# Recurrent scan of a hybrid backbone: both directions' hops side by side, the projection's products in one run behind them

## The chip, the cores and the metric

The kernel runs on one core of a Trainium2 chip. The metric is the device time of one execution in microseconds (us); the median of several runs is compared. Four engines matter here: TensorE (PE in the profile) multiplies, VectorE (DVE), ScalarE (ACT) and GpSimd (POOL) work elementwise, and SyncE's queue (SP) issues most DMAs. Every engine works through its own instructions in order and waits at an instruction until what it needs is there.

## The reference, cut to what matters

One layer of a diffusion backbone over 256 context tokens and 2048 latent tokens (2304 in all, width 1024): a token mixer with three head groups fed by one input projection, then a mixture of experts. The stage that changes is the second head group, a bidirectional RWKV-7 recurrence with 4 heads and a 64x64 state for each head:

```python
def step(S, inp):
    r_t, w_t, k_t, v_t, kk_t, a_t = inp
    sa = -jnp.einsum('nhvk,nhk->nhv', S, kk_t)
    S = S * w_t[:, :, None, :] + sa[..., None] * (kk_t * a_t)[:, :, None, :] + v_t[..., None] * k_t[:, :, None, :]
    return S, jnp.einsum('nhvk,nhk->nhv', S, r_t)
...
y = unboth(_rwkv7_scan(both(r, r), both(w_f, w_b), both(k_f, k_b), both(v, v), both(kk, kk), both(a_f, a_b)))
```

The two directions don't depend on each other. Beside it the input projection `u @ w_in` gives the columns of the two other head groups; those columns are needed only after the scan.

## The kernel before

**The scan.** The 2304 tokens are cut into 18 blocks of 128 for each direction, and `run` (line 609) works through 18 pairs of blocks, one of each direction (d = 0 and 1). A block is four chunks of 32 tokens (u = 0 to 3), and a chunk is a dependent chain of three hops, written in `chunk` (line 646). Hop A multiplies with the masked Gram matrix and the state (lines 652 and 654 on PE, tiles rkGK and rkS), and ACT copies the result out of PSUM (lines 658 and 659, tile rkR). Hop B multiplies with the inverse of the chunk's triangular matrix (line 661, rkTb), and ACT copies again (662 and 663, rkuv). Hop C (666 and, where outputs are needed, 672) gives the update of the state, which VectorE adds (668, rkS); the next chunk's hop A needs it. `chain` (line 624) yields after every hop of every direction: 24 times in a block, n = 0 to 23, even n for direction 0 and odd n for direction 1; chunk, hop and direction run with n like digits.

**The preparation** of the next pair of blocks is a generator of 13 pieces, `prep` (line 494), and `PLAN` (line 623) says behind which n how many of them stand: three behind n = 0, one each behind 1 to 6, 21 and 22, two behind 23. On PE these are four Gram products of 8 PE records each (line 563, tiles rkbk and rkar), each read out of PSUM by four VectorE instructions (567 twice, 569, 570), four transposes (581), read by ACT (583, rkBKt), and, behind n = 21 to 23, the products of the inverse (598 twice, 605 twice). All of them share a ring of two PSUM banks, so a product waits until the one two before it has been read out. Between the Gram products and line 598 lies a chain through other engines: POOL adds (572, rkLc), SP stores and loads (573, 504), VectorE solves the triangular systems in 15 steps of two small instructions (513, 514), SP stores and loads again (517, 588), and POOL expands the result (591, rkD).

**The filler products.** Behind each hop `fill` issues some of the projection's products; they need nothing of the scan. `FILL[n//2%3]` is how many: 4 behind hop A, 3 behind B, 4 behind C. They are lines 184 (128x384 results) and, for columns that go by token, 203 (128x256); 24 of them make one result, which ACT and VectorE take out of PSUM (188 or 800 to 808; 207 and 208) and SP stores. The weights are loaded by SP (162) and split by ACT (163) and POOL (164, tile wl). The activations come in thirds, and at the start of a new third they are loaded through POOL's queue (line 145).

**What sets the order.** PE's instructions stand as the program issues them in this stage (`manual_schedule`, line 1756). Those of the other engines, and everything behind the scan, are placed by a scheduler that plans with its own model of the times; a change of PE's order can so move rows on any engine.

Of the kernel before, what the change touches and what calls it, by code (L numbers as in the profile page):

```python
# [460 lines left out]
class Rwkv:  # L461
# [147 lines left out]
    def run(s, L, fill):  # L609

        s.loads(L[0])
        for n,_ in enumerate(s.prep(L[0])): fill(-1,n)
        for i,segs in enumerate(L):
            nxt=L[i+1] if i+1<len(L) else None
            P=iter(())
            if nxt: s.loads(nxt); P=s.prep(nxt)
            K=s.PLAN.copy()
            for n,_ in enumerate(s.chain(segs,i>=2)):
                for _ in range(K.pop(n,0)): next(P,None)
                fill(i,n)  # L620
            for _ in P: pass

    PLAN={0:3,1:1,2:1,3:1,4:1,5:1,6:1,21:1,22:1,23:2}
# [1059 lines left out]
                    s.finish((15-b)*128,f,sm)  # L1683


PRE=250; PREP={7:200}; FILL=(4,3,4)

R0=dict(g=(0,1),mm=(2,3,4),a0=(5,),a1=(6,),c=(7,)); RG=dict(g=(0,1),mm=(2,3),a0=(5,),a1=(6,),c0=(7,),c1=(4,))
LEAD=3; WO=3; EL=8; PRE0=288
def body(tc, I, out, dbg=None, mark=lambda n: None):  # L1690
    nc=tc.nc; es=ExitStack()
    with es:
# [20 lines left out]
        with P('rp') as rp:  # L1713
# [28 lines left out]
          def fill(k):  # L1742
              for _ in range(k):
                  if next(p2,0)==0: return
# [6 lines left out]
        with P('rkc') as rkc, ExitStack() as e2:  # L1751
# [4 lines left out]
            with pr, tc.manual_schedule(engines={mybir.EngineType.PE}):  # L1756
                fill(PRE)
                mark('scan')
# [99 lines left out]
```

## Time and profile before

| | us |
|---|---|
| median of 3 runs | 3917.51 |
| the 3 runs | 3916.85, 3917.51, 3926.28 |
| the profiled execution | 3949.18 |
| its span, first to last instruction | 3947.4 |
| scan with fillers and preparation, 655 to 1415 us of the span | 760 |
| the stage behind it (SSD and GLA head groups), 1415 to 1900 us | 485 |

The profiled execution lasts 31.7 us longer than the median of the runs without a profile; 1.8 us of its time lie outside its span. In the rows of a timeline the first number is the start in us from the span's start, the second the duration, and a bracket at the end gives the idle time of that engine before the row and what ended it. Rows of equal instructions that follow each other are merged, and xN is their count; one product of 32-bit floats in 128 columns shows as two PE records, so hop B is x2.

### The profile page before, as it was taken

The page shows a single profiled execution, that of the slowest core. Times are in us where ns is not written, and L with a number is a line of the kernel's source. Part 1 is how long each engine was busy: PE and PEld are TensorE (multiplying, and loading weights), DVE is VectorE, ACT ScalarE, POOL GpSimd, SP SyncE. Part 2 cuts the span into 40 slices and gives each one's busy share as a digit, 9 for nine tenths or more (in the row PEclk, how much of TensorE's full clock was granted, in tenths as well). Part 3 has the DMA queues.
Part 4 walks back from the last instruction along what each step waited for, and adds up shares of the span by engine and source line. Part 5 has one row for each costly group of instructions (what it writes and reads, how often), then busy time and mean ns, then how long its engine had stood idle before and what let it go on. Part 6 is the DMA issues. An engine that isn't in the chain of part 4 may idle for free. (4 is left out here: it accounts for less than half of the span.)

```text
span 3947.4 us, 66654 instructions
## 1 busy us (share of the span) xinstructions
PE 3525.1 (89%) x23502; PEld 3006.8 (76%) x23502; DVE 2685.3 (68%) x6775; ACT 1706.2 (43%) x3955; POOL 1329.0 (34%) x1224
## 2 busy tenths in 40 slices
PE   8989887999799978995789899999999999999986
PEld 5978777888688857774567678888888887787865
DVE  4576865876777648775899766666666665666658
ACT  3555553545454533444555323343333333333334
POOL 0243543443343310100044533333334343344323
PEclk9999989999899988996899899999999999999988
DMA  7656554333333276864665468788788887888874
GB/s 228 212 184 206 175 152 133 83 100 101 111 92 98 51 223 215 250 186 167 199 194 167 156 172 231 220 251 243 219 241 242 251 235 227 245 242 229 254 210 160
DMA packets 498511, 745.81 MB, mean 189 GB/s; under 512 B 156704, under 2 KB 393312, under 8 KB 469216
## 3 DMA queue, kind: packets, MB, share of 16 engines
q1 hardware_dynamic: 438880, 522.20, 41.0%
q0 software_dynamic: 59296, 219.33, 22.0%
q8 instruction: 187, 3.06, 0.3%
q14 instruction: 148, 1.21, 0.1%
HBM read 524.31 MB, written 217.06 MB: 188 GB/s over the span
## 5 line engine op out<-in xcount | busy, mean ns | idle before, releaser
L1546 POOL DMA_INDIRECT d_f<-yo,en x162 | 346.6, 2140 | 569.4 <-DVE yo L1543 314.0
L1543 DVE SCALAR_TENSOR_TENSOR yo<-mm,f_w,g2r 128x512 f32<-128x512 f32 (+7 forms) x324 | 236.6, 744 | 265.6 <-PE mm L1541 171.2
L1562 POOL DMA_INDIRECT xg<-d_h,en x162 | 232.1, 1433 | 371.8 <-DVE yo L1543 61.6
L184 PE MATMUL b<-uh,wh 128*128 128x384 f32 (+1 forms) x912 | 320.1, 356 | 12.6 <-ACT sce L805 5.2
L184 PE MATMUL b<-ul,wh 128*128 128x384 f32 (+1 forms) x912 | 320.3, 352 | 5.9 <-DMA ul<-d_ul 3.6
L184 PE MATMUL b<-uh,wl 128*128 128x384 f32 (+1 forms) x912 | 320.9, 352 | 0.0
L1445 DVE TENSOR_TENSOR w13l<-raw,w13h 128x2048 fp32r<-128x2048 f32 x102 | 232.8, 2283 | 25.3 <-ACT w13h L1445 25.3
L1445 ACT ACTIVATE w13h<-raw 128x2048 fp32r<-128x2048 f32 x102 | 195.0, 1914 | 104.5 <-DMA raw<-in_exp_w_dram 94.4
L1328 POOL DMA_INDIRECT d_tab<-q_tk,q_slot x128 | 146.9, 1148 | 248.2 <-DVE q_slot L1321 135.7
L1541 PE MATMUL mm<-w2h,hWh 128*128 128x512 f32 (+7 forms) x480 | 202.3, 422 | 13.0 <-DVE yo L1543 12.3
L1512 PE MATMUL a<-w13h,xTh 128*128 128x512 f32 x464 | 190.2, 410 | 9.0 <-ACT xTh L1471 8.4
L1445 DVE TENSOR_TENSOR w2l<-raw,w2h 128x2048 fp32r<-128x2048 f32 x66 | 151.3, 2293 | 68.9 <-ACT w2h L1445 66.0
L1512 PE MATMUL a<-w13l,xTh 128*128 128x512 f32 x464 | 190.4, 410 | 8.0 <-DVE w13l L1445 8.0
L1541 PE MATMUL mm<-w2h,hWl 128*128 128x512 f32 (+7 forms) x480 | 186.9, 404 | 6.8 <-DVE hWl L1504 6.8
L1541 PE MATMUL mm<-w2l,hWh 128*128 128x512 f32 (+7 forms) x480 | 191.2, 399 | 1.6 <-DVE w2l L1445 1.6
L184 PEld LDWEIGHTS b<-uh,wh 128*128 128x128 f32 x912 | 175.9, 194 | 20.2 <-ACT sce L805 6.4
L1512 PE MATMUL a<-w13h,xTl 128*128 128x512 f32 x464 | 187.7, 405 | 0.0
L184 PEld LDWEIGHTS b<-ul,wh 128*128 128x128 f32 x912 | 177.7, 195 | 9.3 <-DVE ul L139 4.0
L184 PEld LDWEIGHTS b<-uh,wl 128*128 128x128 f32 x912 | 177.6, 195 | 1.4
L1445 ACT ACTIVATE w2h<-raw 128x2048 fp32r<-128x2048 f32 x66 | 126.5, 1916 | 116.1 <-DMA raw<-in_exp_w_dram 70.5
L1475 PE MATMUL g<-ident,xg 128*128 128x128 f32 (+9 forms) x1296 | 167.6, 263 | 9.9 <-DMA xg<-d_h,en 5.8
L1475 PEld LDWEIGHTS g<-ident,xg 128*128 128x128 f32 (+9 forms) x1296 | 142.4, 140 | 38.2 <-issue 14.6
(706 smaller groups left out, 10553.8 us busy)
## 6 DMA issues: line engine op xcount, KB each, us to landing
raw<-in_exp_w_dram SPq DMA_DIRECT2D x162, 1024.0 KB
w13h<-in_exp_w_dram SPq DMA_DIRECT2D x30, 1024.0 KB
wr<-in_w_in_dram SPq DMA_DIRECT2D x46, 512.0 KB
uht<-d_uh POOLq DMA_DIRECT2D x32, 512.0 KB
ult<-d_ul POOLq DMA_DIRECT2D x32, 512.0 KB
mrw<-in_ada_w_dram SPq DMA_DIRECT2D x32, 512.0 KB
rkX<-d_ops SPq DMA_DIRECT2D x36, 384.0 KB
rpx<-d_rw SPq DMA_DIRECT2D x54, 192.0 KB
```

Of the source, the lines that this page charges most:

```text
L184: s.nc.tensor.matmul(P.rearrange("p (i t)->p i t",t=128),l,r[:,a//128:,k],start=(i==0),stop=(i==23)); i+=1
L1328: d=s.nc.gpsimd.indirect_dma_start(out=s.S['tab'],out_offset=bass.IndirectOffsetOnAxis(ap=s.slot[:,l,k:k+1],axis=0),in_=s.tk[:,l:l+1],in_o ...
L1445: pin(nc.scalar.activation(H,r,AF.Copy)); pin(nc.vector.tensor_tensor(L,r,rnd(H),op=OP.subtract))
L1475: for k in range(4): nc.tensor.transpose(p[:,k,:m],B['x'][:m,(4*g+k)*128:(4*g+k+1)*128],s.id[:m,:m])
L1512: nc.tensor.matmul(p,a[:,k],b[:,:,k],start=(i==0),stop=(i==23)); i+=1
L1541: nc.tensor.matmul(r[:m],a[:,k],b[:,k,cs],start=(i==0),stop=(i==5)); i+=1
L1543: else: nc.vector.scalar_tensor_tensor(o[:m,cs],r[:m],B['w'] if isinstance(B['w'],float) else B['w'][:m],s.g2[:m,cs],op0=OP.mult,op1=OP.mult)
L1546: d=nc.gpsimd.indirect_dma_start(out=s.S['f'],out_offset=bass.IndirectOffsetOnAxis(ap=B['en'][:m],axis=0),in_=o[:m],in_offset=None,compute ...
L1562: s.nc.gpsimd.indirect_dma_start(out=x[:m],out_offset=None,in_=s.S['h'],in_offset=bass.IndirectOffsetOnAxis(ap=B['en'][:m],axis=0))
```

## The change

The fillers now stand only behind the odd n, that is behind the hop of direction 1, twice as many at a time: 8 behind the two hops A, 6 behind the two hops B, 8 behind the two hops C. Their number in a chunk (22) and in a block (88) is as before. `PLAN` and the pieces of the preparation are as before.

```diff
             for n,_ in enumerate(s.chain(segs,i>=2)):
                 for _ in range(K.pop(n,0)): next(P,None)
-                fill(i,n)
+                if n%2: fill(i,n)
             for _ in P: pass
...
-PRE=250; PREP={7:200}; FILL=(4,3,4)
+PRE=250; PREP={7:200}; FILL=(8,6,8)
```

First place, PE in the 16th block, chunk u = 3, hop A of both directions (652 and 654: the hop; 203: fillers). Before:

```order
L652 MATMUL b_14018<-rkuv_5463,rkGK_13594 64x64 x2
L654 MATMUL b_14018<-rkS_5468,rkar_5447 128x128 x2
L203 MATMUL b_14358<-wh,uh 128x256
L203 MATMUL b_14358<-wl,uh 128x256
L203 MATMUL b_14358<-wh,ul 128x256
L203 MATMUL b_14358<-wh,uh 128x256
L652 MATMUL b_14019<-rkuv_5465,rkGK_13631 64x64 x2
L654 MATMUL b_14019<-rkS_5472,rkar_5449 128x128 x2
```

And after:

```order
L652 MATMUL b_14018<-rkuv_5463,rkGK_13594 64x64 x2
L654 MATMUL b_14018<-rkS_5468,rkar_5447 128x128 x2
L652 MATMUL b_14019<-rkuv_5465,rkGK_13627 64x64 x2
L654 MATMUL b_14019<-rkS_5472,rkar_5449 128x128 x2
L203 MATMUL b_14368<-wh,uh 128x256
L203 MATMUL b_14368<-wl,uh 128x256
L203 MATMUL b_14368<-wh,ul 128x256
L203 MATMUL b_14368<-wh,uh 128x256
```

Direction 1's hop moved up past four fillers; eight now follow.

Second place, PE in the same chunk, from hop B of direction 1 to the second product of line 598 (rkD is what POOL's line 591 makes). Before:

```order
L661 MATMUL b_14021<-rkR_14370,rkTb_13992 128x128
L598 MATMUL b_14434<-rkD,rklf_5455 128x128 x4
L203 MATMUL b_14358<-wh,ul 128x256
L203 MATMUL b_14358<-wh,uh 128x256
L203 MATMUL b_14358<-wl,uh 128x256
L666 MATMUL b_14020<-rkuv_5463,rkBKt_13670 128x128 x2
L672 MATMUL b_14018<-rkuv_5463,rkGK_13594 64x64 x2
L598 MATMUL b_14450<-rkD,rklf_5457 128x128 x4
```

And after:

```order
L661 MATMUL b_14021<-rkR_14361,rkTb_13972 128x128
L598 MATMUL b_14431<-rkD,rklf_5455 128x128 x4
L203 MATMUL b_14368<-wh,ul 128x256
L203 MATMUL b_14368<-wh,uh 128x256
L203 MATMUL b_14368<-wl,uh 128x256
L203 MATMUL b_14368<-wh,ul 128x256
L203 MATMUL b_14368<-wh,uh 128x256
L203 MATMUL b_14368<-wl,uh 128x256
L666 MATMUL b_14020<-rkuv_5463,rkBKt_13663 128x128 x2
L672 MATMUL b_14018<-rkuv_5463,rkGK_13594 64x64 x2
L598 MATMUL b_14450<-rkD,rklf_5457 128x128 x4
```

The three fillers that stood ahead of direction 1's hop B and of the first product of line 598 stand behind it now.

Third place, VectorE in the 8th block (the last third of the activations is loaded there), behind the last read of a Gram product (570). Before:

```order
L570 TENSOR_TENSOR rkGK_10048<-b_10065,mgk_5426 128x512
L549 TENSOR_TENSOR rkbk_5451<-rkX,rkEi 64x4x32 x2
L668 SCALAR_TENSOR_TENSOR rkS_5468<-b_9932,rkG_9459,rkSG_9938 128x64 x2
L549 TENSOR_TENSOR rkbk_5451<-rkX,rkEi 64x4x32 x2
L668 SCALAR_TENSOR_TENSOR rkS_5472<-b_9933,rkG_9489,rkSG_10034 128x64 x2
L533 SCALAR_TENSOR_TENSOR rkA<-rm_5434,rkX 128x128 x2
```

And after:

```order
L570 TENSOR_TENSOR rkGK_10039<-b_10065,mgk_5426 128x512
L533 SCALAR_TENSOR_TENSOR rkA<-rm_5434,rkX 128x128 x2
L549 TENSOR_TENSOR rkbk_5451<-rkX,rkEi 64x4x32 x2
L668 SCALAR_TENSOR_TENSOR rkS_5468<-b_9932,rkG_9459,rkSG_9938 128x64 x2
L549 TENSOR_TENSOR rkbk_5451<-rkX,rkEi 64x4x32 x2
L668 SCALAR_TENSOR_TENSOR rkS_5472<-b_9933,rkG_9489,rkSG_10025 128x64 x2
```

Line 533, which reads a freshly loaded tile (rkX), moved ahead of both directions' updates of the state. In the order of the stage behind the scan some rows of PE, VectorE, ACT and SP stand elsewhere too.

## Rows read from the trace of the kernel before

**Rows 1.** Busy time by stretch: us of the stretch, then for each engine its busy us and its count, the granted clock of TensorE as a share of 2.4 GHz, the DMA share and GB/s.

```profile
655.00:1415.00 760.00, 684.42 (x5349) 609.84 (x5347) 546.00 (x1645) 382.44 (x1240) 286.20 (x392) 0.97 0.34 88
1415.00:1900.00 485.00, 380.61 (x5088) 306.28 (x5089) 336.68 (x829) 199.92 (x532) 41.79 (x82) 0.85 0.70 219
```

**Rows 2.** The waits of PE between 655 and 1415 us: what waited, for what; us in total, times, longest.

```profile
PE b L598 <- POOL rkD L591: 42.5, 13, 18.6
PE b L661 <- ACT rkR L659: 11.6, 11, 3.1
PE b L581 <- DVE rkGK L570: 10.6, 11, 1.8
PE b L563 <- DVE rkTb L607: 3.5, 4, 1.3
```

**Rows 3.** Timeline of PE, a chunk with 128x256 fillers and nothing of the preparation, hop A of both directions.

```profile
1295.14 0.34 PE L652 MATMUL b<-rkuv,rkGK 128*64 128x64 f32 x4
...
1295.87 0.36 PE L203 MATMUL b<-wl,uh 128*128 128x256 f32 x1
...
1296.19 0.28 PE L203 MATMUL b<-wh,uh 128*128 128x256 f32 x1
1296.31 0.28 PE L203 MATMUL b<-wl,uh 128*128 128x256 f32 x1
1296.52 0.34 PE L652 MATMUL b<-rkuv,rkGK 128*64 128x64 f32 x4
```

**Rows 4.** The same with 128x384 fillers.

```profile
1037.91 0.34 PE L652 MATMUL b<-rkuv,rkGK 128*64 128x64 f32 x4
...
1038.64 0.42 PE L184 MATMUL b<-ul,wh 128*128 128x384 f32 x1
1038.90 0.34 PE L184 MATMUL b<-uh,wl 128*128 128x384 f32 x1
1039.08 0.35 PE L184 MATMUL b<-uh,wh 128*128 128x384 f32 x1
...
1039.53 0.34 PE L652 MATMUL b<-rkuv,rkGK 128*64 128x64 f32 x4
```

**Rows 5.** Timeline of PE in the last block, where the fillers have run out and the hops of both directions stand side by side.

```profile
1400.88 0.29 PE L652 MATMUL b<-rkuv,rkGK 128*64 128x64 f32 x4
...
1401.74 0.34 PE L652 MATMUL b<-rkuv,rkGK 128*64 128x64 f32 x4
...
1403.32 0.49 PE L661 MATMUL b<-rkR,rkTb 128*128 128x128 f32 x2 [0.38 <-ACT rkR L659]
```

**Rows 6.** Timeline of PE around the first and the second product of line 598, in four blocks.

```profile
1006.18 2.07 PE L598 MATMUL b<-rkD,rklf 128*128 128x128 f32 x8 [18.55 <-POOL rkD L591]
...
1270.43 0.82 PE L598 MATMUL b<-rkD,rklf 128*128 128x128 f32 x5 [0.71 <-POOL rkD L591]
...
1345.20 1.16 PE L598 MATMUL b<-rkD,rklf 128*128 128x128 f32 x8 [1.45 <-POOL rkD L591]
1346.11 0.36 PE L203 MATMUL b<-wh,ul 128*128 128x256 f32 x1
...
1346.55 0.61 PE L666 MATMUL b<-rkuv,rkBKt 128*128 128x128 f32 x4
...
1388.08 2.08 PE L598 MATMUL b<-rkD,rklf 128*128 128x128 f32 x8 [8.42 <-POOL rkD L591]
```

**Rows 7.** Timelines of PE and VectorE from the first Gram product to the second transpose of a block.

```profile
1352.90 1.95 PE L563 MATMUL b<-rkar,rkbk 128*128 128x128 f32 x16
...
1361.17 0.63 PE L581 MATMUL b<-ident,rkbk 128*128 128x128 f32 x4
...
1353.99 0.57 DVE L567 TENSOR_TENSOR rkLb<-b,mlo 32x128 f32<-32x128 f32 x2 [1.18 <-PE b L563]
...
1360.33 0.69 DVE L570 TENSOR_TENSOR rkGK<-b,mgk 128x512 f32<-128x512 f32 x1
```

**Rows 8.** Timelines of PE and ACT around the products of line 605 in the 7th block: ACT copies the second product of line 598 out (600, rkW), which the second half of the x16 needs.

```profile
948.02 2.17 PE L605 MATMUL b<-rkD,rkW 128*128 128x128 f32 x16
...
948.40 0.58 ACT L600 ACTIVATE rkW<-b 128x512 f32<-128x512 f32 x1
```

**Rows 9.** Timelines of the 8th block, where the last third of the activations is loaded: the SP queue (durations are those of issuing), then VectorE, then PE.

```profile
955.31 0.38 SPq L489 DMA_DIRECT2D rkX<-d_ops  x1
...
956.30 6.28 SPq L162 DMA_DIRECT2D wr<-in_w_in_dram  x1
...
965.73 1.29 SPq L573 DMA_DIRECT2D rkLd<-rkLc  x2
...
960.98 0.48 DVE L668 SCALAR_TENSOR_TENSOR rkS<-b,rkG,rkSG 128x64 f32<-128x64 f32 x2
...
967.92 0.74 DVE L533 TENSOR_TENSOR_SCAN rkA<-rm,rkX 128x128 f32<-128x128 f32 x2 [5.09 <-DMA rkX<-d_ops]
...
969.58 0.49 PE L661 MATMUL b<-rkR,rkTb 128*128 128x128 f32 x2 [3.02 <-ACT rkR L659]
```

**Rows 10.** Timelines of VectorE and POOL: a step of the triangular solve alone, one beside a product of POOL, and that product.

```profile
983.46 0.20 DVE L513 TENSOR_TENSOR rktm<-rkSy,rkTn 64x55 f32<-64x55 f32 x1
...
983.93 2.27 DVE L513 TENSOR_TENSOR rktm<-rkSy,rkTn 64x60 f32<-64x60 f32 x1
...
983.74 2.39 POOL L164 TENSOR_TENSOR wl<-wr,wh 128x1024 fp32r<-128x1024 f32 x1 [12.12 <-issue]
```

## The prediction

> **What bounds the kernel now.** The change touches one stage, so I read that stage first: which engine is busy, and what PE waits for when it isn't. Between 655 and 1415 us PE is busy 684 of 760 us at a granted clock of 0.97, and VectorE 546 us [rows 1]. The reader should see two things: PE is the fullest engine, and about 76 us of the stage are PE's waits. The table of waits then says where these lie [rows 2]: 42.5 us before the products of line 598, 11.6 us before hop B, 10.6 us before the transposes, 3.5 us before the first Gram product of a block. So the hops, which the change brings together, hardly wait: their fillers cover the copies between them. What waits is the preparation of the next block. Line 598 waits 13 times. One of these is a second product of its block (0.71 us) and one lies in the block where the fillers have run out (8.42 us) [rows 6]; in the other 11 cases the first product stands in PE's order before POOL's expansion is done. Eleven of the 16 blocks that have fillers throughout are therefore paced, up to that product, by the chain over VectorE, SP and POOL and not by PE's work; I call them the paced blocks. The 8th block holds the one long wait, 18.55 us [rows 6].
>
> **The change part by part.** The number of products, copies and DMAs is the same; only PE's order is edited, and with it the places that the scheduler gives to the others.
>
> (a) Hops side by side. With 128x256 fillers, from the start of direction 0's hop A to that of direction 1's takes 1296.52 - 1295.14 = 1.38 us, four fillers among them at a step of 1296.31 - 1296.19 = 0.12 us, so 0.90 us without the fillers [rows 3]. With 128x384 fillers it is 1.62 us, and 0.90 us without four at 0.18 us [rows 4]. Where the fillers have run out the same two hops stand 1401.74 - 1400.88 = 0.86 us apart [rows 5]. Going from hop to filler and back thus costs 0.04 us. Of the 12 pairs of hops in a block, 7 become truly adjacent (behind n = 0, 2, 4, 6 and 22 a piece of the preparation still stands between the two), so 7 x 0.04 = 0.28 us a block, 4.5 us over 16 blocks at most. All seven lie ahead of the first product of line 598, so in the paced blocks the wait takes this up; in the 5 others it counts: 1.4 us, and I take **-1.0**, since hops B and C have no 64-column tile at their start and should save less. The bound below is -4.5.
>
> (b) The cover of the copies. Direction 1's copies for hop B queue behind direction 0's on ACT; without fillers that shows as a wait of 0.38 us before direction 1's hop B [rows 5]. Before, four fillers, hop B of direction 0 and three fillers covered them; now eight fillers and that hop. From one hop of a direction to its next there are 6 to 8 fillers and one hop of the other direction, before and after, at 0.12 to 0.18 us each. So the new neighbourhood costs **nothing**, because 8 x 0.12 = 0.96 us hide 0.38. If that cover were gone, it would be 0.38 us in 4 chunks of 16 blocks, 24 us.
>
> (c) Pieces of the preparation behind odd n. They used to follow fillers of the same pair and now come ahead of them: the third Gram product by 4 fillers, the first transpose by 3, the third by 4, the first product of line 598 by 3, both of line 605 by 4. The pieces behind even n keep their place. Gram products and transposes: from the first Gram product to the second transpose passes 8.27 us in a block, and VectorE's reading out fills it from 1353.99 to 1361.02 [rows 7]; the second transpose is what waits (10.6 us in 11 cases [rows 2]) and there are 14 fillers ahead of it before and after. So the third Gram product will wait a little earlier for its bank, and the sum stays; bound 0 to +2.4 (0.15 us in 16 blocks).
>
> The first product of line 598 is different: in the paced blocks it starts when POOL is done, whatever stands ahead of it, and work moved from before it to behind it is added to the block. Three fillers move: 3 x 0.12 = 0.36 or 3 x 0.18 = 0.54 us, 0.45 in the mean (the three that stand behind it already, with the way into hop C, take 1346.55 - 1346.11 = 0.44 us [rows 6]), in 11 blocks: **+4.8** at 0.44, bound 0 if the chain should end earlier by as much. The second product gains these three fillers as cover, so its one wait of 0.71 us shrinks: **-0.4**.
>
> The products of line 605 lose four fillers of distance to the second product of line 598, whose copy by ACT they need. In the 7th block that copy ends at 948.98 and the second half of the x16 starts at about 949.0 [rows 8], so there the 0.48 us are lost, in most blocks not; **+0.5**, bound 0 to +1.
>
> (d) Behind line 605 stand eight fillers where there were four, so the next block's first Gram product comes later against VectorE's reading of its bank: 3.5 us in 4 waits [rows 2], of which up to 0.6 us each go: **-2.4**, bound -3.5.
>
> (e) Other engines. In the 8th block VectorE's order puts line 533 ahead of both updates of the state. It waited 5.09 us for its tile until 967.92 us, while the updates had run at 961 [rows 9]. If the tile lands as late again, the next hop A can start only at about 967.92 + 0.74 + 0.48 us and a small product, 970 us, where before hop B of that chunk came at 969.58, behind a wait of 3.02 us [rows 9]: some 3 us lost. If the tile lands in time, because the order of POOL now has the big load a little later, the 3.02 and 0.4 us behind it go. I take **0**, with -3.4 to +3.
>
> The sum: -1.0 + 4.8 - 0.4 + 0.5 - 2.4 + 0 = **+1.5 us** on the profiled execution's 3949.18, so 3950.7; carried to the median of the runs, 3917.51 + 1.5 = **3919.0**.
>
> One rule of the Trainium skill bears on the chain that paces the blocks. A step of the solve takes 0.20 us; the one that runs beside POOL's product of 2.39 us takes 2.27 us and ends where that product ends [rows 10]. The Trainium skill, SBUF — State Buffer, section SBUF: two separate sides, says that VectorE instructions with two SBUF inputs and GpSimd's share a port pair as an exclusive lock, held for the whole instruction; the trace agrees with it here. By that rule the sum would keep its terms and gain one, the number of such meetings more or fewer times 2.07 us; I leave it at zero and make it a rival.
>
> **The rivals.**
>
> R1, slower: POOL's product meets the solve more often. A meeting lengthens the chain by 2.27 - 0.20 = 2.07 us [rows 10], and in a paced block PE waits all of it. It decides from the point at which line 164 starts while the 15 steps run. For it: POOL's and VectorE's rows are placed anew, with the two updates of the state close together. Against: the scheduler moved few of POOL's rows. One meeting more in half of the paced blocks is 12 us: 3919 + 12 = 3931; in all of them 3942.
>
> R2, faster: the 8th block's long wait shrinks. The stores of line 573 stood on SP behind a weight load that took 6.28 us to issue and left at 965.73 [rows 9]. If they leave with the others, the solve begins about 9 us earlier, and with the wait of 3.02 us some 12 us of the 18.55 + 3.02 go: 3907. Against: the solve also stands behind the fillers' own VectorE work in that block.
>
> R3, either way: the stage behind the scan is laid out anew. PE is idle 485 - 381 = 104 us there [rows 1]; a tenth to an eighth of that won or lost is 10 to 13 us: 3907 or 3931. Nothing in the trace gives the sign.
>
> R4: the edit gives what its shape suggests, 24 runs of fillers becoming 12, each change worth the 0.04 us of (a) with nothing lost at line 598: -4.5 - 2.4, 3911. The paced blocks speak against it; it counts with the forecast, as no measurable change.
>
> **How the numbers follow.** A measurement of this kernel can tell about 0.3% from no change, that is 11.8 us: 3905.8 to 3929.3. The forecast with R4 and the small misses of each term have 0.55. R1 has 0.15 and R3 on that side 0.09: slower 0.24. R2 has 0.13 and R3 on that side 0.08: faster 0.21, the greater part of it close to the edge. The range adds the bounds: below -4.5 - 3.5 - 3.4 and a part of R2 or R3, 3902; above 4.8 + 2.4 + 1 + 3 and R1 in half the blocks or R3, 3939. R1 in all blocks and a loss of all cover lie outside.
>
> **What would show it.** Steps (a) and (b): two hops A 0.86 us apart, and waits before hop B not above some 15 us in all. Step (c): line 598 still the longest wait, 45 to 50 us in about 12 cases, and some waits now at line 605 and at the third Gram product. Step (d): the waits of line 563 for rkTb near 1 us. The stage would end at 1415 + 1.5 us. The prediction is wrong if hop B's waits grow to tens of us (the cover of (b) was misjudged), if line 598's waits change by more than 10 us (R1, R2), or if the stage behind the scan changes its length by as much (R3).

## The result, and the profile after

The changed kernel takes 3968.77 us in the median of 4 runs (3963.17 to 3991.37), the kernel before 3921.90 us beside it: the ratio is 1.0131, 95% interval 1.0086 to 1.0175, 47 us slower. The prediction was 3919 with a range up to 3939.

The same two stretches as in [rows 1], after (the scan, then the stage behind it; columns as there):

```profile
649.70:1426.70 777.00, 690.99 (x5347) 619.59 (x5346) 545.32 (x1643) 382.59 (x1239) 285.02 (x392) 0.95 0.33 86
1426.70:1924.30 497.60, 387.55 (x5089) 312.20 (x5087) 337.13 (x827) 201.04 (x532) 41.79 (x82) 0.82 0.68 214
```

The scan is 17.5 us longer than before (759.55, from the first hop to the last) and the stage behind it 12.8 us longer (484.80). PE's waits in the scan, as in [rows 2]:

```profile
PE b L598 <- POOL rkD L591: 58.8, 14, 25.9
PE b L581 <- DVE rkGK L570: 10.8, 11, 2.6
PE b L666 <- ACT rkuv L663: 7.2, 6, 3.2
PE b L661 <- ACT rkR L659: 3.9, 11, 0.5
```

Line 598 has 16 us more than before, hop B (661) 8 us less, and hop C (666), which waits for the copies behind hop B, 7.2 us instead of 3.1. Where no piece of the preparation stands, a chunk can take as long as before: here the one that answers to [rows 3], PE's timeline from its first hop A to that of the next chunk.

```profile
1306.18 0.34 PE L652 MATMUL b<-rkuv,rkGK 128*64 128x64 f32 x4
...
1307.09 0.34 PE L652 MATMUL b<-rkuv,rkGK 128*64 128x64 f32 x4
...
1312.88 0.34 PE L652 MATMUL b<-rkuv,rkGK 128*64 128x64 f32 x4
```

It takes 1312.88 - 1306.18 = 6.70 us; before, the same chunk (from 1295.14) took 6.68. The scan's loss is to be looked for where the preparation stands. By groups of blocks (1 to 7, the 8th, 9 to 16), a second execution of the kernel before:

```profile
654.20:949.40 295.20, 274.47 (x2123) 247.46 (x2122) 220.49 (x672) 153.34 (x493) 122.62 (x165) 0.97 0.33 83
949.40:1014.50 65.10, 42.58 (x313) 37.84 (x312) 33.17 (x95) 20.52 (x66) 21.06 (x30) 0.79 0.54 165
1014.50:1352.10 337.60, 317.44 (x2499) 282.79 (x2498) 262.10 (x756) 177.69 (x571) 133.94 (x187) 0.99 0.33 83
```

And after:

```profile
649.70:954.70 305.00, 276.29 (x2122) 250.61 (x2121) 222.13 (x673) 152.93 (x493) 121.96 (x165) 0.97 0.32 81
954.70:1020.40 65.70, 39.71 (x315) 35.76 (x314) 30.14 (x94) 21.66 (x69) 20.64 (x29) 0.79 0.53 163
1020.40:1365.50 345.10, 324.21 (x2497) 290.23 (x2496) 261.71 (x754) 176.83 (x568) 134.29 (x187) 0.98 0.32 81
```

The loss is spread: 9.8 us in the first seven blocks, most of it idle time of PE, 0.6 in the 8th, 7.5 in the blocks 9 to 16, most of it busy time at a lower granted clock.

The start of the first product of line 598 parts each of the 17 blocks that hold a preparation in two. Summed over these blocks, by the starts in the traces, 612.2 us lie ahead of it and 128.3 from it to the block's end in the second execution of the kernel before; in the changed kernel 616.3 and 142.1, in its second execution 620.3 and 142.2. So 13.9 us of the scan's loss lie behind that product in both executions, and 4.1 and 8.1 ahead of it. Most blocks have 0.3 to 0.9 us more behind it, the 2nd has 1.8, the 4th and the 11th have 2.9 each. Chunk by chunk (each from its first hop A to that of the next), the changed kernel's two executions take -0.7 and -0.4 us more in the first chunks of these blocks, 1.4 and 1.8 in the second, -4.2 and -4.2 in the third, 21.7 and 25.1 in the fourth, which holds lines 598 and 605. The 11th block grew most, from 44.8 to 50.9 us (49.6 in the second execution). Its first product of line 598, and the stretch from there to its end in the columns of [rows 1], in the kernel before (second execution):

```profile
1138.31 1.16 PE L598 MATMUL b<-rkD,rklf 128*128 128x128 f32 x8 [1.72 <-POOL rkD L591]
...
1138.31:1145.82 7.51, 7.51 (x59) 6.89 (x60) 5.97 (x13) 4.16 (x12) 3.74 (x5) 1.00 0.33 86
```

And after:

```profile
1146.65 2.08 PE L598 MATMUL b<-rkD,rklf 128*128 128x128 f32 x8 [3.74 <-POOL rkD L591]
...
1146.65:1157.04 10.39, 10.39 (x63) 9.61 (x63) 4.47 (x14) 4.21 (x12) 4.00 (x6) 0.75 0.19 50
```

Behind the longer wait a part of the stretch ran at the lower of TensorE's two clock levels, 1.2 GHz; before, all of it ran at 2.4 GHz.

**A table for what follows.** From the traces: the scan (first hop A to last hop C), the stage behind it, and the router's stretch behind that (first product of line 1237 to the last of line 1366: the output projection and the choice of experts), in us. The first row of results is the kernel before, run again (e1_before_again); each ratio is to the kernel before on the same chip.

| run | ratio | scan | stage | router |
|---|---|---|---|---|
| kernel before | | 759.55 | 484.8 | 371 |
| e1_before_again | 0.9995 (0.998 to 1.001) | 759.06 | 486.3 | 370 |
| changed kernel | 1.0131 (1.0086 to 1.0175) | 777.06 | 497.6 | 373 |
| e6_after_again | 1.0135 (1.0113 to 1.0158) | 781.15 | 499.5 | 387 |
| e2_pieces_back | 1.0088 (1.0062 to 1.0115) | 783.42 | 492.1 | 373 |
| e3_pieces_only | 1.0090 (1.0063 to 1.0118) | 787.26 | 497.5 | 361 |
| e4_pairs_lean | 1.0134 (1.0108 to 1.0159) | 778.80 | 499.2 | 400 |
| e5_one_block | 1.0045 (1.0028 to 1.0062) | 759.14 | 498.4 | 374 |
| e12_other_block | 1.0038 (1.0021 to 1.0055) | 759.85 | 494.2 | 387 |
| e8_products_first | 1.0138 (1.0118 to 1.0158) | 766.75 | 494.3 | 405 |
| e7_weights_first | 1.0136 (1.0114 to 1.0159) | 783.86 | 494.1 | 391 |
| e9_weights_ahead | 1.0131 (1.0103 to 1.0159) | 774.25 | 492.2 | 391 |
| e11_fifth_block | 1.0019 (1.0001 to 1.0036) | 772.85 | 480.0 | 368 |
| e10_l598_back | 1.0088 (1.0061 to 1.0114) | 777.63 | 502.2 | 366 |
| e13_behind_kept | 1.0083 (1.0062 to 1.0104) | 782.46 | 486.7 | 371 |
| e16_shortest_behind | 0.9998 (0.9986 to 1.0009) | 762.80 | 487.6 | 364 |
| e14_all_kept | 1.0056 (1.0040 to 1.0072) | 781.16 | 486.9 | 367 |
| e15_pieces_kept | 1.0033 (1.0018 to 1.0047) | 775.85 | 490.3 | 372 |
| e17_copies_free | 1.0012 (0.9994 to 1.0030) | 766.40 | 486.4 | 358 |
| e18_copies_free_all | 1.0045 (1.0029 to 1.0061) | 776.79 | 485.5 | 353 |

For the changed kernel run again, the three stretches are 22.1 + 13.2 + 16.9 = 52.2 us longer than in e1, and the timed medians (3997.15 and 3939.16) differ by 58.0, the ratio of 1.0135 being 53. For the first pair the three stretches give 17.5 + 12.8 + 2 = 32 us of 47, or 33 against e1; the rest was not found. What lies behind the router's stretch came at 1664 to 1687 us in these traces, at 1676 and 1665 in the two executions of the kernel before, and is left out. So two things are to be explained, the scan and what lies behind it.

### The profile page after: what moved, and what is told of

Same layout as the page of the kernel before. It is cut to its first block, busy times and chain, and to the rows that moved or that the text cites. A ratio compares the mean times of both kernels' runs of the same rounds, so it can differ in the third digit from the quotient of the medians.

```text
span 3972.1 us, 66644 instructions
## 1 busy us (share of the span) xinstructions
PE 3532.2 (89%) x23502; PEld 3017.7 (76%) x23502; DVE 2692.2 (68%) x6775; ACT 1709.5 (43%) x3955; POOL 1332.6 (34%) x1224
## 5 line engine op out<-in xcount | busy, mean ns | idle before, releaser
L1562 POOL DMA_INDIRECT xg<-d_h,en x162 | 242.4, 1496 | 377.9 <-PE mm L1541 73.3
```

The source lines that it names most:

```text
L1562: s.nc.gpsimd.indirect_dma_start(out=x[:m],out_offset=None,in_=s.S['h'],in_offset=bass.IndirectOffsetOnAxis(ap=B['en'][:m],axis=0))
```

## The experiments

**Kernels run unchanged.** They show how far the stretches repeat.

> The kernel before once more, nothing edited: a second profiled execution, and the scatter of a comparison of equals. All theories: ratio 1.000 within 0.3%. If the 31.7 us by which the first profiled execution exceeded the median come from taking the profile, this one is near 3949 us again with a scan near 759 us and a stage behind it near 484 us; if they were chance, it is nearer to 3920 us and the same two stretches show where the excess lay. The long wait of the 8th block (18.55 us) shows whether it is a fixture (15 to 22 us) or chance.

> The changed kernel once more, nothing edited: a second profiled execution on the same chip as the others. If its scan (777.1 us), its stage (497.6 us) and its long wait (25.9 us) are properties of its layout, they come again within 2 us; if they were chance, they differ by more. The ratio is 1.010 to 1.015.

The scan and the stage repeat to 0.5 and 1.5 us for the kernel before, to 4.1 and 2.0 for the changed one; the router's stretch of the changed kernel came at 373 and 387 us. So a few us of scan or stage are read with care, and the router's stretch only where the timed runs bear it out.

**Halves of the edit.** e2 keeps the pairs but puts the pieces behind odd n back between the two halves of a run; e3 moves only the pieces, and with them ahead of direction 1's hop, which the change does not; e4 makes the pairs only where no piece stands.

```diff
 e2, against the changed kernel
-                for _ in range(K.pop(n,0)): next(P,None)
+                [fill(i,n) for _ in range(n%2)]; [next(P,None) for _ in range(K.pop(n,0))]
-FILL=(8,6,8)
+FILL=(4,3,4)
 e3, against the kernel before
-                for _ in range(K.pop(n,0)): next(P,None)
+                for _ in range(K.pop(n,0)+(K.pop(n+1,0) if n%2==0 else 0)): next(P,None)
 e4, against the kernel before
-                fill(i,n)
+                for _ in range(1 if not 8<=n<20 else 2*(n%2)): fill(i,n)
```

> Hops paired as in the changed kernel, but the run of fillers behind a pair is split in two halves and the pieces of the preparation that belong to the odd n stand between the halves, so each has as many fillers ahead of it as before. Theory T1 (the pieces came too early, term c): the scan returns to 755 to 762 us from 776.8, the waits at line 598 to some 42 us, the time to about 3920 to 3930. Theory T3 (the pairing itself costs, terms a and b): the scan stays at 772 to 778 us. Theory T2 (the stage behind the scan is laid out anew by any change of the order): the stage behind the scan differs from 484 us by some 5 to 15 us either way, whatever the scan does.

> The kernel before with its hops and fillers where they were, but the pieces of the preparation that belong to an odd n issued ahead of the fillers behind the even n in front of it, that is 3 or 4 fillers earlier, which is term c alone. T1: the scan gets longer by 10 to 18 us, with line 598 waiting near 59 us. T3: the scan stays within 4 us of 759. T2: the stage behind the scan differs from 484 us by 5 to 15 us either way.

> Fillers paired as in the changed kernel only behind n = 8 to 19, where no piece of the preparation stands; the rest as before. So only terms a and b act, on half of the pairs, and no piece moves against the fillers. T1: the scan is 756 to 760 us, within 3 of before. T3: about half of the growth, 764 to 770 us. T2: the stage behind the scan differs from 484 us by 5 to 15 us either way although no piece moved.

All three are slower than the kernel before, by 0.9 to 1.3%, each alone about as much as the whole, and none of the three scans lies where T1 or T3 had it. The parts don't add up. In e2 and e4 one block makes much of it: the 8th takes 75.4 and 76.7 us, 65.1 in e1; without it e4's scan is 8 us longer than e1's, near the half that T3 gave. And each of these kernels has a stage behind the scan of 492 to 499 us, though none of its code was touched.

**The stage behind.** e5 and e12 pair the hops in one block only, the 15th and the 4th.

```diff
-                fill(i,n)
+                for _ in range(1 if i!=14 else 2*(n%2)): fill(i,n)
```

> The fillers paired only in one block of the eighteen, the fifteenth; every other hop, filler and piece of the scan stands as in the kernel before. T2 (the scheduler lays the stage behind the scan out anew after any edit, and the layout of before is better than most): the scan stays at 759 us within 1.5, and the stage behind it takes 490 to 500 us where before's takes 484.8 and 486.3; the time is 0.1 to 0.4% longer. Rival T5 (the stage gets longer because the scan ran otherwise, not because of the layout): with the scan unchanged the stage stays within 2 us of 486 and the ratio within 0.1% of 1.

> The fillers paired only in the fourth block, all else as in the kernel before: a second edit of about one eighteenth of the change. T2: the scan stays within 3 us of 759, and the stage behind it and the stretch of the router are laid out anew: the stage 490 to 500 us, the router's stretch anywhere from 360 to 405 us, the time 0.2 to 1.2% longer. Rival (the fifteenth block was an unlucky place): the stage is at 484 to 488 us, the router's stretch at 368 to 373 us and the ratio within 0.15% of 1.

The scan and the stage of e5:

```profile
652.00:1411.10 759.10, 684.83 (x5347) 610.35 (x5346) 550.25 (x1644) 381.59 (x1239) 285.32 (x392) 0.96 0.34 88
1411.10:1909.60 498.50, 392.15 (x5090) 317.65 (x5087) 338.08 (x827) 201.16 (x532) 41.70 (x82) 0.82 0.68 214
```

One block's pairing leaves the scan where it was and costs 12 us behind it against e1, with 9 us more of busy PE at a clock of 0.82: the scheduler lays the later rows out anew. To separate the order from the scan that precedes it, e13 is the changed kernel with the rows behind the scan held, on all engines, in the order of the kernel before. ORDER lists that order, and each row gets an edge of order alone to the one ahead of it (class B: rows behind the scan).

```diff
+CHAIN=lambda e,c: 'B' if c=='B' else None
-        n=nc.values_load(s.nit[0:1,0:1],min_val=0,max_val=s.OV//s.U)
+        pinned(s.tc); n=nc.values_load(s.nit[0:1,0:1],min_val=0,max_val=s.OV//s.U)
```

> The changed kernel, but all rows of all engines behind the scan are held in the order that they have in the kernel before; the scan is laid out as in the changed kernel. T2 (the layout makes the time behind the scan): the stage takes 484 to 489 us and the router's stretch 368 to 374 us as before, the scan 777 to 783 us, the ratio is 1.004 to 1.007. Rival T5 (these stretches get longer because the scan before them ran otherwise): the stage takes 492 to 500 us with the old order too, and the ratio stays above 1.008.

```profile
653.80:1436.20 782.40, 694.23 (x5347) 622.92 (x5346) 545.38 (x1643) 382.74 (x1239) 284.81 (x392) 0.95 0.33 86
1436.20:1922.90 486.70, 381.22 (x5088) 307.65 (x5087) 336.40 (x827) 200.06 (x532) 41.78 (x82) 0.85 0.70 219
```

Behind the changed kernel's longer scan the stage now takes 486.7 us, as before, at the clock of [rows 1]. With the old order held, the stage's loss is gone, within the 2 us by which it repeats. The ratio fell less than was expected, to 1.0083, with a scan of 782.5. The layouts that these edits happened to get lie between 480.0 and 502.2 us; e16 tests whether the shortest (that of e11) is a gain by itself, behind the unchanged scan.

> The kernel before, its scan untouched on all engines, with the rows behind the scan in the order of the shortest layout seen so far (stage 480.0, router's stretch 368.3 us). T2: the scan 759 us, the stage 479 to 482 us, the router's stretch 367 to 371 us, the ratio 0.997 to 0.999, below both kernels. Rival: the stage is at 485 us or more since it was short only behind that scan.

The stage came at 487.6 and the time at 0.9998: T2 missed here. The same rows in the same order took 480.0 us behind e11's scan and 487.6 behind this one, so the order is not all that sets the stage's length; what else does was not found. It is no faster kernel.

**The 8th block.** Its wait before line 598 grew from 18.55 us [rows 6] to 25.92. SP's weight load (162), POOL's big loads (145) and the two small loads of the solve's result (588), from the timelines of SP, POOL and ACT in the kernel before (second execution), then of SP, POOL, ACT and PE after:

```profile
984.52 0.38 SPq L162 DMA_DIRECT2D wr<-in_w_in_dram  x1
...
999.98 1.00 SPq L588 DMA_DIRECT2D rkDT<-rkTd  x2
...
986.47 0.59 POOL L145 DMA_DIRECT2D uh<-d_uh  x1
...
989.13 1.06 ACT L163 ACTIVATE wh<-wr 128x1024 fp32r<-128x1024 f32 x1 [2.66 <-DMA wr<-in_w_in_dram]
```

```profile
987.42 0.39 SPq L162 DMA_DIRECT2D wr<-in_w_in_dram  x1
...
1002.66 0.39 SPq L162 DMA_DIRECT2D wr<-in_w_in_dram  x1
1003.17 1.72 SPq L588 DMA_DIRECT2D rkDT<-rkTd  x2
...
986.00 0.59 POOL L145 DMA_DIRECT2D uh<-d_uh  x1
...
999.16 1.06 ACT L163 ACTIVATE wh<-wr 128x1024 fp32r<-128x1024 f32 x1 [14.47 <-DMA wr<-in_w_in_dram]
...
1009.83 2.08 PE L598 MATMUL b<-rkD,rklf 128*128 128x128 f32 x8 [25.92 <-POOL rkD L591]
```

Before, the weight load left ahead of the big loads and was there after 989.13 - 984.52 = 4.6 us, when ACT's split began; after, it left behind them and took 999.16 - 987.42 = 11.7. The next weight load needs the buffers that this chain frees, and the solve's loads stand behind it on SP. In the Trainium skill, DMA: Bandwidth & Descriptors, section Queues, rings and completion order, each DMA engine takes packets in turn from the queues that have work; the two durations agree with that.

e8 makes only POOL's swap in the kernel before (its four products of line 551 ahead of the weight split 164); e7 takes the swap back in the changed kernel; e9 also puts SP's weight load ahead of a store.

```diff
 e9, against the changed kernel (e7: without the part with ZS; e8: the edge of split turned round, in the kernel before)
+def behind(x,w): TC[0].add_manual_dep(x.ins,w.ins.name,mybir.DependencyInfo(mybir.DependencyClass.NoSync,mybir.DependencyReason.DATA),reason='order')
+def split(w): WL.append(w); [behind(AR[a],w) for a in range(72,76) if len(WL)==30]
-                    nc.sync.dma_start(wr[:,:,o:o+n],wi[:,q+m*j:q+m*j+m,c0:c0+n]); o+=n
+                    w=nc.sync.dma_start(wr[:,:,o:o+n],wi[:,q+m*j:q+m*j+m,c0:c0+n]); o+=n; keep or bufs<3 or len(WL)!=30 or behind(ZS[21],w)
```

> The kernel before with only that pair of POOL's rows swapped in the 8th block: line 551 ahead of the split of the weights (line 164); PE's order in the scan is unedited. T6: the long wait grows from 18.8 to 25 to 28 us and the scan from 759 to 766 to 771 us, although no hop and no filler moved. Rival: both stay within 2 us. The stage is laid out anew here too; T2: 487 to 500 us; T5: within 2 us of 486 unless the scan's end shifts it.

> The changed kernel with one pair of POOL's rows swapped back in the 8th block: the split of the weights (line 164) ahead of the four products of line 551, as it stands in the kernel before; PE's order in the scan is that of the changed kernel. Theory T6 (this swap makes the long wait: SP loads the next weights only when line 164 is done, so they now leave behind the 3 MB of line 145, and line 588 stands on SP behind a weight load that waits for them): the long wait before line 598 falls from 25.9 to 18 to 20 us and the scan from 777 to 767 to 772 us. Rival (the long wait comes from when the fillers call for the last third of the activations): it stays at 25 to 27 us. The stage behind the scan is laid out anew again; T2 lets it lie anywhere from 485 to 500 us.

> The changed kernel with two rows of the 8th block put back as in the kernel before: on POOL line 164 ahead of line 551, and on SP the weight load (162) that waits for it ahead of one store of line 211. Theory T7 (what decides is whether that weight load leaves ahead of the 3 MB of line 145 or behind them): the load leaves before line 145's, the wait before line 598 falls from 25.9 to 18 to 20 us, and the block's end comes 4 to 8 us earlier, the scan at 771 to 777 us. Rival T8 (the long wait is set by when the fillers run into the last third, the order of the queues only names another row): the wait stays at 25 to 27 us. The stage behind the scan is one more layout: 490 to 500 us by T2.

e8: the load leaves at 991.38, behind the big loads at 989.75; the wait is 24.8 us and the scan 7.7 us longer, from one swap. e7, against its expectation: 25.6, unchanged, because SP still issued the weight load behind a store, at 996.33, and the big loads had left at 994.93. e9: the load left at 986.10, ahead of the big loads at 988.09, the wait is 20.1 and the block 59.2 us long instead of 65.7. e2 and e4 fit too: the load leaves behind the big loads, and the waits are 26.9 and 27.3 us; in e3 it leaves ahead, and the wait is 19.3. So the order of the loads sets this wait; POOL's swap matters where it turns that order. With the loads in their old order the changed kernel's 8th block is 5.9 us shorter than e1's 65.1. But the scan as a whole fell only to 774.25, and the time not at all: the layout behind was another again.

e11 is e9 with two rows of the 5th block moved, POOL's 591 and SP's 588 ahead of what had come to stand before them.

```diff
+ ... (len(WL)==26 and behind(w,DT[11]))
+ ... 49<=len(AR)<=52 and behind(AR[-1],DI[10])
```

> The kernel of the run before with the 8th block's weights ahead, and in the 5th block too the rows of two queues as in the kernel before: on POOL the first product of line 591 ahead of the four of line 551 (which wait for a hop of PE), on SP the loads of line 588 ahead of a 512 KB weight load (162). PE's order in the scan is that of the changed kernel. If the growth of the 5th block (41.2 us before, 45.3 and 45.5 in the changed kernel) comes from these places in the queues, the block takes 41 to 43 us and the scan 770 to 772 us instead of 774.3. Rival (the block grows because its solve and its hops share VectorE otherwise): it stays at 44.5 to 46 us and the scan within 1.5 us of 774. The stage behind the scan is one more layout.

The 5th block did not shrink (47.8 us; 45.5 in e9, 41.2 in e1), so neither its theory nor its rival held. The ratio of 1.0019 comes from the stage behind, 480.0 us, and was not foreseen.

**The first product of line 598.** e10 puts it back behind three of the six fillers that it had been moved ahead of; fill(i,25) issues three, by an edit that is not shown here.

```diff
-                for _ in range(K.pop(n,0)): next(P,None)
-                if n%2: fill(i,n)
+                if n==21: fill(i,25)
+                [next(P,None) for _ in range(K.pop(n,0))]; n%2 and fill(i,25 if n==21 else n)
```

> The changed kernel with only the first product of line 598 put back behind three of the six fillers that it had been moved ahead of; every other row of PE in the scan as in the changed kernel. It measures the term that was put at +4.8 us: by the prediction the time from that product to the block's end shrinks by 0.44 us in each block, 6 to 7 us over all and about 5 us where the product waits, so the scan takes 771 to 776 us instead of 777 to 781. Rival (the product gains nothing by its place, since the wait is only renamed): the scan stays within 2 us of 777 to 781. The stage is one more layout: 490 to 500 us by T2.

From that product to the end of the block the blocks' sum fell from 142.2 us to 129.6, by 12.6 us, but the time ahead of it grew from 616.3 (620.3 in e6) to 629.4, and the scan stayed at 777.6. With every engine's rows free to move, a part of the edit could not be priced.

**PE's order alone.** e14 has the changed kernel's PE order in the scan and every other row of the program in the order of the kernel before. e15 is the same with the PE order of e2, that is the pairs without the moved pieces.

```diff
+CHAIN=lambda e,c: (None if c!='B' else 'B') if e=='PE' else 'A'
```

> The changed kernel's order of PE in the scan, and every other row of the program, on every engine, held in the order of the kernel before. This is what the prediction's sum speaks of, +1.5 us with nothing else moved. If the sum is right the scan takes 757 to 764 us, the stage 484 to 489 us, and the ratio is 0.999 to 1.002. If PE's own order costs what the scan lost, the scan takes 770 to 783 us and the ratio is 1.003 to 1.007. A third case: the old order suits the new hops worse than the scheduler's new one (copies and filler results wait for each other), then the scan is above 783 us.

> As the run before, every row but PE's in the scan held in the order of the kernel before, and on PE the pieces of the preparation stand behind as many fillers as before (half of the run of fillers, the pieces, the other half). By the prediction term c goes: the scan is 4 to 7 us shorter than that of the run with all kept, 752 to 758 us if that is at 760, and the ratio 0.998 to 1.000. If the pieces' place is worth nothing, both scans agree within 2 us.

The scans of e14 and of e15, from the table by stretch:

```profile
653.90:1435.10 781.20, 698.21 (x5347) 624.26 (x5346) 543.03 (x1644) 382.22 (x1239) 286.37 (x392) 0.95 0.33 86
```

```profile
653.30:1429.10 775.80, 694.44 (x5347) 622.43 (x5346) 544.88 (x1643) 382.32 (x1239) 285.53 (x392) 0.95 0.33 86
```

The loss stays in the scan with all other orders held: it belongs to PE's order, or to that order against the old ones of the other engines, which e17 and e18 take up. The moved pieces are worth 781.16 - 775.85 = 5.3 us, the pairs 775.85 - 759.06 = 16.8, each from one execution. Of these, 8.1 us are busy time of PE (694.44 against 686.36 in e1) and 8.6 are waits, 6.1 of them before hop B. How hop B comes to wait shows in the 14th block of e15, timelines of ACT and of PE:

```profile
1263.24 1.06 ACT L163 ACTIVATE wh<-wr 128x1024 fp32r<-128x1024 f32 x1 [0.57 <-PE b L184]
1264.20 0.47 ACT L188 ACTIVATE fo<-b 128x384 f32<-128x384 f32 x1
1264.57 0.20 ACT L658 ACTIVATE rkR<-b 64x64 f32<-64x64 f32 x1
...
1261.96 0.71 PE L654 MATMUL b<-rkS,rkar 128*128 128x128 f32 x4
...
1263.04 0.34 PE L184 MATMUL b<-uh,wl 128*128 128x384 f32 x1
...
1265.06 0.49 PE L661 MATMUL b<-rkR,rkTb 128*128 128x128 f32 x2 [0.98 <-ACT rkR L659]
```

Direction 1's hop A is through at 1262.67, but its copies (658) stand on ACT behind a weight split and a read-out of a filler result, and these wait for fillers of line 184 that stood ahead of the hop before and stand behind it now. The eight fillers behind the hop can't cover that, for they are what is waited for. The 5th block of e15 shows the other half, in the timelines of PE and VectorE and then in the table by stretch:

```profile
855.24 0.61 PE L666 MATMUL b<-rkuv,rkBKt 128*128 128x128 f32 x4
...
855.96 0.47 DVE L668 SCALAR_TENSOR_TENSOR rkS<-b,rkG,rkSG 128x64 f32<-128x64 f32 x2 [2.93 <-PE b L666]
```

```profile
844.80:855.00 10.20, 10.20 (x47) 9.52 (x47) 5.32 (x21) 3.96 (x15) 2.16 (x5) 0.50 0.10 32
```

PE ran there at the lower of its two clock levels, 1.2 GHz, for 10.2 us that e1 ran at the higher one, behind a wait at line 581 of 1.29 us that both kernels have. Half of 10.2 is 5.1 us, and the block's first two chunks are 5.2 us longer. Not all of that need be the edit's: behind the same wait the first execution of the kernel before ran 3.4 us at 1.2 GHz and the second none. In the middle of the solve VectorE stood 2.93 us before the update of the state, until the late hop C.

e17 and e18 are e15 and e14 with ACT's order in the scan left to the scheduler, which puts direction 1's copies ahead of 163 and of the read-outs.

```diff
-CHAIN=lambda e,c: (None if c!='B' else 'B') if e=='PE' else 'A'
+CHAIN=lambda e,c: (None if c!='B' else 'B') if e in('PE','Activation') else 'A'
```

> The order of ACT in the scan is left to the scheduler; PE's order and every other row are those of e15 (pairs, pieces back between the halves of a run). What moves on ACT: direction 1's copies out of hop A (658, 659) stand again ahead of the weight split (163) and of the read-outs of filler results (800, 805, 807), which wait for fillers that now come behind that hop. Theory A (step (b) failed on ACT: the copies of direction 1 are held up behind rows that wait for the moved fillers): waits before hop B fall from 17.3 us to 8 or less, and the scan from 775.9 us to 767 to 770. Rival B (the blocks are paced by the preparation's chain and by the half clock, and the time won before hop B is waited out elsewhere): waits before hop B fall as much, but those at lines 598, 581 and 666 grow, and the scan stays at 774 to 778. Either way the stage behind stays at 485 to 491 us, its order being held.

> The same with the PE order of the change as it was made (that of e14): only ACT's order in the scan is free. Theory A: waits before hop B fall from 13.7 us to 6 or less and the scan from 781.2 us to 773 to 776. Rival B: they fall as much, and the scan stays at 779 to 783, as it did with the change itself (3.9 us of waits before hop B, scan 777.1 and 781.2).

The 14th block of e17 on ACT, then PE's waits in the scan of e17 and that scan by stretch:

```profile
1253.34 0.22 ACT L658 ACTIVATE rkR<-b 64x64 f32<-64x64 f32 x1
1253.57 0.22 ACT L659 ACTIVATE rkR<-b 64x64 f32<-64x64 f32 x1
1253.87 1.06 ACT L163 ACTIVATE wh<-wr 128x1024 fp32r<-128x1024 f32 x1
1254.95 0.49 ACT L188 ACTIVATE fo<-b 128x384 f32<-128x384 f32 x1
```

```profile
PE b L598 <- POOL rkD L591: 48.6, 13, 19.8
...
PE b L661 <- ACT rkR L659: 8.8, 15, 3.0
```

```profile
652.50:1418.90 766.40, 685.57 (x5347) 614.23 (x5346) 550.95 (x1643) 382.44 (x1239) 284.82 (x392) 0.96 0.34 87
```

Hop B's wait in the 14th block is gone, hop B waits 8.8 us in all instead of 17.3, the 10.2 us at 1.2 GHz in the 5th block shrink to 3.4, and the scan is 9.5 us shorter, 766.4, with PE's busy time back at 685.6. The second chunks of the 17 blocks take 150.2 us; in e15 161.6, in e1 147.1. Theory A holds for the pairs alone, within a us of its numbers. Rival B has a part: line 598 waits 6 us more than in e15, and 7.3 us of the 16.8 remain, from one execution of a scan that repeats to 4.1 us in the changed kernel. The timed ratio of 1.0012 flatters this kernel, its router's stretch being 358 us by the trace. e18's scan is 776.8, 4.4 us shorter than e14's and just above what theory A gave; so with ACT free the moved pieces cost 776.79 - 766.40 = 10.4 us. This lies behind the first product of line 598: from there to the blocks' ends 144.6 us in e18, 127.2 in e17.

## Why the prediction was wrong

Two of the prediction's own signs of being wrong came: line 598's waits changed by 16.3 us and the stage behind the scan by 12.8, where 10 was the limit for each. The third did not: hop B's waits fell.

**What failed first: the sum ended with the scan.** The prediction's terms stop at the last hop and carry zero for what stands behind. R3 named the mechanism and its size (10 to 13 us either way) and had 0.17 in all. The runs showed it right: 11 to 13 us of the loss are the stage laid out anew (e5, e13). The router's stretch behind it, which no rival spoke of, had 17 more in one of two executions; in the old order (e13, e14, e15, e17, e18) it came at 353 to 372 us, so how much of that is the order is not shown. "Nothing in the trace gives the sign" still holds; of the eleven orders of PE or POOL tried with the stage free to be laid out anew, ten got 492 to 502 us and one 480.

**Step (b), the cover of the copies, was argued wrongly.** "So the new neighbourhood costs nothing, because 8 x 0.12 = 0.96 us hide 0.38" counted the fillers on PE and not the rows on ACT that wait for those fillers and stand ahead of the copies. With ACT's order as it was, this and the lower clock behind it cost 9.5 us (e15 against e17). With ACT laid out anew, as in the changed kernel, hop B waits only 3.9 us there, as (b) said, though hop C waits 4.1 more; and pairing still costs 7.3 us of scan (e17). In the changed kernel itself this failing is not what cost the time: its second chunks take 148.5 us, 1.4 more than e1's, where e15's take 14.5 more. Line 598 waits 8.2 us more in e17 than in e1 (48.6 against 40.4), and its first product starts 8.3 us later in the blocks' sum (620.5 against 612.2). The solve on VectorE ends 6.2 us later in that sum, 3.0 of them in the 8th block; what holds it up was not settled.

**Step (a)** was worth nothing: hops A now stand 1307.09 - 1306.18 = 0.91 us apart instead of the 0.86 that was expected, and the chunk takes 6.70 against 6.68. The -1.0 was too much, but small.

**Step (c)** had the right sign and was mis-sized: it is the term of the scan that failed. It put +4.8, with -0.4 and +0.5, on the time behind the first product of line 598, and that time grew by 13.9 us in both executions. The 0.3 to 0.9 us of most blocks are about the size of the moved fillers. What the term left out is the lower clock behind a longer wait, as in the 11th block (2.9 us there and in the 4th), and the wait before line 605 in the 2nd (1.02). With all else held the term is 5.3 us (e14 against e15), and 6.6 behind that product; but the 5.3 hold an 8th block that came 6.2 us shorter, so the match with the forecast is in part luck. With ACT free it is 10.4 (e18 against e17), which its bounds did not hold. That it can't be had back piece by piece, e10 showed.

**Steps (d) and (e)** held. The waits of line 563 for rkTb, 3.5 us in [rows 2], are gone; line 605 has one wait, of 1.02 us. VectorE's line 533 [rows 9] started at 963.77 without a wait, the good end of (e), and hop B's wait of 3.02 us went; but the block's long wait took 7.4 us more through the order of the loads, and the block ended at +0.6.

**The rivals.** R1 did not happen: of the steps of the solve (513 and 514) ten in the scan of e1 and nine of the changed kernel took longer than 1.2 us [rows 10]. Of R2 the first half came, and not by the stores of line 573: in the 8th block the solve began 1.3 us earlier and ended 8.1 us earlier after the block's start (35.6 us against 43.7 in e1). But SP's weight load held the loads of its result back, and the wait grew; where that load left early (e9), the block was 5.9 us shorter. R4 gave no 0.04 us for a change between hop and filler, as step (a) shows.

**The sum as measured.** Pairs 7.3, moved pieces 10.4: 17.7 us, the scan of e18 against e1; the changed kernel's own scan, whose other engines stand in another order, has 18.0 and 22.1, so how close these come is not proof of the two shares. Layout of the stage 11 to 13; the router's stretch 3 to 17, its cause not shown. Against e1 that makes 33 and 52 by the traces, for 47 and 53 by the ratios.

## What to carry to other kernels

Where products are moved past a step of a critical chain, list on every other engine the rows that wait for those products and stand ahead of that chain's rows: the moved work is no cover for a copy that is queued behind its own read-out. Where a scheduler places the rest of the program, price an edit with the rest held in its old order before crediting or blaming it: here the edit of one block, or one swap, moved the time by 0.4 to 1.4%. Price work that moves behind a long wait at the clock that rows behind such a wait show: here 10.39 us for 7.51. And a short stretch that one layout happens to give is not a gain until it has been put behind the kernel that is to keep it.

## What the runs showed of the hardware

A 512 KB load (128x1024 values of 4 bytes) on SP's queue took 4.6 us when it left 2 us ahead of the big loads on POOL's queue and 11.7 us when it left 1.4 us behind the first of them. Behind the same wait of 1.29 us at the same product the granted clock fell to 0.50 for 10.2 us in one kernel (e15), and in the kernel before for 3.4 us in one execution and not in the other. The stage behind the scan, with the same instructions, took 484.8 to 490.3 us in its old order, at a mean granted clock of 0.83 to 0.85, and in the eleven new ones 480.0 to 502.2, at 0.81 to 0.84; one order gave both 480.0 and 487.6.
